# A two-layer hybrid encoder trunk on one core: output sums and combinations placed behind the newest low part on VectorE, ScalarE's final scalings spaced out, token tile 2 updated on VectorE

## The chip, the cores and the metric

The kernel runs on 1 core of one Trainium2 chip. The metric is device microseconds of an execution. TensorE (PE) multiplies, VectorE (DVE) and ScalarE (ACT) prepare operands and finish results, GpSimd (POOL) and SyncE (SP) mostly issue DMAs. Each engine takes its instructions strictly in the order in which they are queued on it.

## The reference

Two layers work on x of 512 tokens by 2048 features, float32. Cut to what matters:

```python
def hybrid_layer(x, w_in, w_out, g_pre, g_post, w_alpha, b_alpha, g_gla, g_att, rel_bias):
    h = rmsnorm(x, g_pre)
    z = h @ w_in                      # 2048 x 7184
    ...                               # gated linear attention, chunked attention, gates
    y = jnp.concatenate([o_gla, o_att], axis=-1) @ w_out     # 2048 x 2048
    return x + rmsnorm(y, g_post)

def reference(x, ...):
    h = x
    for l in range(2):
        h = hybrid_layer(h, w_in[l], w_out[l], ...)
    return h
```

The change concerns the output projection `@ w_out`, its RMS normalisation and the residual addition at the end of a layer.

## The kernel before

**Precision by splitting.** Every float32 operand is split into a high part (a cast to float32r) and a low part (the operand minus its high part). A product is three matmuls: high by high, high by low, low by high. For weights ScalarE makes the high part `wh` (line 191) and VectorE the low part `wl` (line 199). For activations and their sums the helper `split` does the same (cast at line 105 on ScalarE, low part at line 106 on VectorE).

**Seven products for eight.** Most projections use a Strassen-like scheme over 2 x 2 blocks with seven products P1 to P7 (`fast_gemm`). A projection of a pair of 512-column weight blocks is 28 jobs: a product and one of four chunks of 256 features, such as "52", product P5 of chunk 2. The order of the jobs is a list in the code; for the first output pair it is `PROD_OUT`. A job loads its weight block by a SyncE DMA (`raw` or `H`), some add or subtract two blocks on VectorE (lines 185 and 187), then `wh` and `wl` follow, and TensorE runs 12 matmuls of 128x512 (line 381). In the first output pair the jobs run 10 20 11 21 12 13 50 51 60 61 22 23 52 53 62 63 30 31 32 33 70 71 72 73 40 41 42 43. There are 4 buffers for `raw` and for `wh`, and 3 for `wl`.

**The other side's sums.** The products P5, P6, P3 and P7 need sums of activation blocks, named S1, S2, S4 and S3. For the output projection they are made by the generator `output_sums`: S1, S2 and S3 are differences (`sub`, line 1136), S4 is a sum (line 1153); `put` splits each (lines 105 and 106) and, in the last layer, GpSimd writes it to memory, from where the second output pair loads it again.

**Finishing.** As products complete, `combine` (line 338) forms an output block from accumulators and kept copies (line 333), and `project` squares it on ScalarE (line 1280) and multiplies it by the gain on VectorE (line 1281). After the second pair of the last layer `finish_token` does each of the four token tiles: a sum of squares (line 1296), a power on GpSimd (line 421), then the scaled result plus the residual `x_mid`. For tiles 0 and 1 and the first half of tile 2, ScalarE scales in place (line 1305), a GpSimd DMA adds `x_mid` into the tile (line 1306), and SyncE writes it out (line 1307). The second half of tile 2 and tile 3 are done by one VectorE instruction each piece (line 1311) and written from SyncE and ScalarE (line 1313).

**What sets the order.** Program text gives the dependencies; a scheduler in the framework, which works from its own estimate of times, sets the order on each engine. `tc.issue_after(x)` makes an instruction of the block stand behind x in the queue of x's own engine; it is an order, not a wait on a semaphore. `last_cast` holds the newest `wh` cast traced so far. Generators of side work are stepped from inside the matmul loops (`pump`), one step at a time.

Of the kernel before, what the change touches and what calls it, by code (L numbers as in the profile page):

```python
# [10 lines left out]
AF = mybir.ActivationFunctionType  # L11
ALU = mybir.AluOpType
# [21 lines left out]
def hybrid_trunk(  # L34
# [13 lines left out]
    nc = tc.nc  # L48
# [26 lines left out]
    def t2(shape=(512,), dtype=F32):  # L75
        return tmp.tile([P] + list(shape), dtype, tag="t2", name=nm("t2"))
# [55 lines left out]
    PROD_END = order("10 20 11 21 12 22 13 23 50 51 60 52 61 53 62 63 30 31 32 33 70 71 72 73 40 41 42 43")  # L132
    PROD_OUT = order("10 20 11 21 12 13 50 51 60 61 22 23 52 53 62 63 30 31 32 33 70 71 72 73 40 41 42 43")
    LEFT = {"P5": "S1", "P6": "S2", "P3": "S4", "P7": "S3", "P4": "A22"}
    last_cast = [None]

    class Job:
        def __init__(self, l, kind, c, b0, b1=None, pair=None):
# [57 lines left out]
        def low(self):  # L196
            self.wl = rtile("wl", dtype=F32R, bufs=3)
            for z in self.parts():
                nc.vector.tensor_tensor(  # L199
                    out=self.wl[:, z, :], in0=self.src[:, z, :], in1=self.wh[:, z, :].bitcast(F32), op=ALU.subtract  # L200
                )
            if self.kind == "P2" and self.b0 < NB_IN:
                h = self.pair["H", self.c]
                nc.vector.tensor_tensor(out=h, in0=h, in1=self.src, op=ALU.add)
# [483 lines left out]
    def layer(l):  # L688
        last = l == L - 1
# [416 lines left out]
        parts, gains = {}, []  # L1106
# [19 lines left out]
        def output_sums():  # L1126
            def put(name, i, src, tag=None):
                op = O[name, i] = slot(tag, [2, 512], F32R) if tag else rtile("sa", (2, 512), F32R)
                with tc.issue_after(last_cast[0]):
                    split(op[:, 0, :], op[:, 1, :], src)  # L1130
                if last:
                    nc.gpsimd.dma_start(so_d[name, OC[i]], flat(op))
                    written.add((id(so_d), name, OC[i]))

            def sub(dst, a, b):
                nc.vector.tensor_tensor(out=dst, in0=a, in1=b, op=ALU.subtract)

            for i0 in (0, 2):
                for name in ("S1", "S2"):
                    for i in (i0, i0 + 1):  # L1140
                        while (1, OC[i]) not in og:
                            yield
                        a11, _, a21, a22 = parts[OC[i]]
                        sub(a22, *((a21, a22) if name == "S1" else (a22, a11)))
                        put(name, i, a22, None if i0 else f"g{i + 2 * (name == 'S2')}")
                        yield
            for name in ("S4", "S3"):
                for i in range(4):
                    while (("P5", "P6")[i // 2], i % 2 + 2 * (name == "S3")) not in used or (0, OC[i]) not in og:
                        yield  # L1150
                    a11, a12, a21, a22 = parts[OC[i]]
                    if name == "S4":
                        nc.vector.tensor_tensor(out=a12, in0=a12, in1=a22, op=ALU.add)
                        put(name, i, a12, f"g{i}")
                    else:
                        sub(a11, a11, a21)
                        put(name, i, a11)
                    yield
# [135 lines left out]
        def finish_token(t, xs):  # L1294
# [5 lines left out]
            for i in range(D // step):  # L1300
                h, o = i * step // 1024, i * step % 1024
                yt = ys[t, h][:, o : o + step]
                rows = slice(t * P, (t + 1) * P), slice(i * step, (i + 1) * step)
                if last and (t < 2 or (t == 2 and i == 0)):
                    nc.scalar.activation(yt, yt, AF.Copy, scale=r)
                    nc.gpsimd.dma_start(yt, x_mid[rows], accum_op=ALU.add)
                    nc.sync.dma_start(out[rows], yt)
                else:
# [18 lines left out]
        def out_consume(n):  # L1327
# [4 lines left out]
            def f(j, h, t, src, comb):  # L1332
                until(lambda: len(gains) == 2)
                o = 2 * h + t
                project(o, n + j, comb(t2()), gains[j])
                if last and n == 2:
                    if (j, h, t) == (1, 0, 1):
                        tasks.append(finish(0, xs[0]))
# [82 lines left out]
```

## Time and profile before

| what | value |
|---|---|
| median of 3 runs | 1648.65 us (1648.48 to 1649.47) |
| the profiled execution | 1642.34 us, its span 1640.5 us |
| PE busy | 1617.2 us, 99% of the span |
| DVE busy | 1253.5 us, 76% |
| ACT busy | 909.7 us, 55% |
| granted TensorE clock, mean | 0.995 |

The page gives busy time by engine, the span in 40 slices, the queues, the chain that ended last and the costliest groups. In a timeline row stand start, length, engine, line, operation, output and inputs, and in brackets how long the engine stood idle before it and what ended that. Rows overlap a little: an instruction starts before the one ahead has drained, so the time one instruction takes of its engine is the distance from start to start. Layer 0's first output pair runs from about 648 to 731 us, layer 1's from about 1465 to 1548 us.

### The profile page before, as it was taken

The numbers are of one execution on the slowest core, as the hardware profiler recorded it, in microseconds if no ns is written. First come the engines' busy times: TensorE is split into PE (matmuls) and PEld (weight loads), VectorE is DVE, ScalarE is ACT, GpSimd is POOL, SyncE is SP. The second block draws the span as 40 slices with busy tenths as digits, with TensorE's granted clock in tenths as the row PEclk, the third lists the DMA queues.
The fourth block names the chain that finished last, engine by engine and source line by source line (L and its number), as shares of the span: only waits on it lengthen the run. The fifth ranks groups of instructions, "written<-read, shape, count | busy, mean of one in ns | idle before, by whom it ended". The sixth has DMA issues, their size and how long they took to land.

```text
span 1640.5 us, 24563 instructions
## 1 busy us (share of the span) xinstructions
PE 1617.2 (99%) x8986; PEld 1383.7 (84%) x8986; DVE 1253.5 (76%) x1635; ACT 909.7 (55%) x1498; POOL 134.2 (8%) x196
## 2 busy tenths in 40 slices
PE   9999999999999999999999999999999999999996
PEld 7888999998888778788888889999988877787885
DVE  5977677687787869985786576776777878699876
ACT  7554445566555456654784444455665545476554
POOL 0120000110100110000132000000000001101002
PEclk9999999999999999999999999999999999999998
DMA  9898685885859667486789486858758596786968
GB/s 345 270 357 293 221 302 199 266 298 173 307 192 339 225 220 267 145 296 214 240 282 394 172 311 218 298 189 273 269 183 291 184 327 235 241 282 246 345 224 269
DMA packets 130760, 426.70 MB, mean 260 GB/s; under 512 B 14084, under 2 KB 26756, under 8 KB 130640
## 3 DMA queue, kind: packets, MB, share of 16 engines
q1 hardware_dynamic: 113760, 366.09, 64.9%
q0 software_dynamic: 16304, 57.96, 9.7%
q8 instruction: 71, 1.16, 0.3%
q10 hardware_dynamic: 576, 1.08, 0.2%
q14 instruction: 49, 0.40, 0.1%
HBM read 371.84 MB, written 53.23 MB: 259 GB/s over the span
## 4 chain that ended last, share of the span: by engine, by line
PE 94%; DMA 2%; DVE 2%; issue 1%; ACT 0%; SPq 0%; DVEq 0%; POOL 0%; ACTq 0%
PE mm L381 47%; PE mm L371 19%; PE mm L302 16%; PE ax L891 2%; PE ax L381 2%; DMA raw<-in_w_dram 1%; PE ax L1072 1%; PE ax L874 1%; PE ax L711 1%; PE ax L1044 1%; DVE wl L199 1%; PE ax L855 1%; PE ax L854 1%; PE ax L853 1%; PE ax L1164 0%
## 5 line engine op out<-in xcount | busy, mean ns | idle before, releaser
L381 PE MATMUL mm<-wh,sa 128*128 128x512 f32 x1472 | 479.2, 396 | 1.2 <-ACT wh L191 1.0
L191 ACT CAST wh<-raw 128x1024 fp32r<-128x1024 f32 (+1 forms) x253 | 265.1, 1052 | 242.6 <-PE mm L381 65.2
L199 DVE TENSOR_TENSOR wl<-raw,wh 128x1024 fp32r<-128x1024 f32 (+1 forms) x253 | 306.5, 1216 | 92.7 <-PE mm L381 38.3
L191 ACT CAST wh<-H 128x1024 fp32r<-128x1024 f32 x240 | 251.4, 1050 | 214.8 <-PE mm L381 90.2
L199 DVE TENSOR_TENSOR wl<-H,wh 128x1024 fp32r<-128x1024 f32 x240 | 292.5, 1221 | 88.1 <-PE mm L381 35.8
L381 PEld LDWEIGHTS mm<-wh,sa 128*128 128x128 f32 x1472 | 277.5, 189 | 68.9 <-issue 7.9
L381 PE MATMUL mm<-wl,sa 128*128 128x512 f32 x736 | 289.6, 394 | 4.7 <-DVE wl L199 4.7
L371 PE MATMUL mm<-sa,wh 128*128 128x256 f32 x1280 | 236.7, 285 | 0.0
L381 PE MATMUL mm<-wh,a 128*128 128x512 f32 x608 | 200.5, 394 | 0.0
L371 PEld LDWEIGHTS mm<-sa,wh 128*128 128x128 f32 x1280 | 199.7, 191 | 0.1
L371 PE MATMUL mm<-sa,wl 128*128 128x256 f32 x640 | 181.2, 283 | 0.0
L381 PEld LDWEIGHTS mm<-wl,sa 128*128 128x128 f32 x736 | 139.1, 189 | 33.7 <-DVE wl L199 6.7
L185 DVE TENSOR_TENSOR H<-H,raw 128x1024 f32<-128x1024 f32 x132 | 160.2, 1219 | 8.1 <-DMA raw<-in_w_dram 7.0
L381 PEld LDWEIGHTS mm<-wh,a 128*128 128x128 f32 x608 | 113.2, 188 | 23.3
L187 DVE TENSOR_TENSOR raw<-H,raw 128x1024 f32<-128x1024 f32 x60 | 73.5, 1224 | 68.8 <-DMA raw<-in_w_dram 68.7
L371 PEld LDWEIGHTS mm<-sa,wl 128*128 128x128 f32 x640 | 122.5, 191 | 0.2
L421 POOL TENSOR_TENSOR sm<-sm,mhalf 128x2 f32<-128x2 f32 (+2 forms) x42 | 57.1, 1360 | 791.8 <-DVE sm L901 453.3
L381 PE MATMUL mm<-wl,a 128*128 128x512 f32 x304 | 119.8, 394 | 0.0
L371 PE MATMUL mm<-a,wh 128*128 128x256 f32 x512 | 95.2, 285 | 0.0
L302 PE MATMUL mm<-wh,a 128*128 128x512 f32 x288 | 91.7, 390 | 0.0
L381 PE MATMUL mm<-wh,g 128*128 128x512 f32 x288 | 90.8, 389 | 0.0
L333 ACT COPY ev<-mm 128x512 f32<-128x512 f32 x96 | 56.0, 583 | 56.3 <-PE mm L381 39.5
(237 smaller groups left out, 2428.5 us busy)
## 6 DMA issues: line engine op xcount, KB each, us to landing
raw<-in_w_dram SPq DMA_DIRECT2D x323, 512.0 KB, 4.8
sa<-S SPq DMA_DIRECT2D x184, 512.0 KB, 4.4
H<-in_w_dram SPq DMA_DIRECT2D x60, 512.0 KB, 4.6
sa<-A SPq DMA_DIRECT2D x48, 512.0 KB, 5.9
S<-g POOLq DMA_DIRECT2D x32, 512.0 KB, 9.0
sa<-oS SPq DMA_DIRECT2D x16, 512.0 KB, 4.5
oa<-g POOLq DMA_DIRECT2D x12, 512.0 KB, 6.6
bias<-in_rel_dram SPq DMA_DIRECT2D x16, 256.0 KB, 4.2
```

Source lines behind the costliest of these rows:

```text
L185: nc.vector.tensor_tensor(out=h, in0=h, in1=r, op=ALU.add)
L187: nc.vector.tensor_tensor(out=r, in0=h, in1=r, op=ALU.subtract)
L191: last_cast[0] = nc.scalar.copy(self.wh[:, z, :], src[:, z, :]).ins
L199: nc.vector.tensor_tensor(out=self.wl[:, z, :], in0=self.src[:, z, :], in1=self.wh[:, z, :].bitcast(F32), op=ALU.subtract)
L302: nc.tensor.matmul(pss[o], a(part, kk, o) if callable(a) else a[:, part, t], rhs[:, kk, :], start=(i == 0 and kk == 0 and m == 0), stop=(i ...
L333: nc.scalar.copy(e, src[t])
L371: nc.tensor.matmul(dst, lhs[:, kk, f], a[:, part, tok], start=(fresh and kk == 0 and m == 0 and ft % 2 == 0), stop=(c == 3 and kk == 1 and ...
L381: nc.tensor.matmul(out_ps[t], a[:, part, tok], rhs[:, kk, :], start=(fresh and kk == 0 and m == 0), stop=(c == 3 and kk == 1 and m == 2), ...
L421: nc.gpsimd.tensor_tensor(out=out_r, in0=v, in1=mhalf[:, : v.shape[-1]], op=ALU.pow)
L711: nc.tensor.matmul(ps[0:96, half * 256 : (half + 1) * 256], wga[kt // 10][:, kt % 10, :], op[:, i, (kt % 2) * 256 : (kt % 2 + 1) * 256], s ...
L853: nc.tensor.matmul(ps[:, :n], self.qh[:, t], self.kh[:, :n], start=True, stop=False)
L891: nc.tensor.matmul(o, self.pt[i][:, j * P : (j + 1) * P], av[hd // 4, j // 2][:, j % 2, (hd % 4) * P : (hd % 4 + 1) * P], start=(j == 0), ...
```

## The change

Five edits. `last_low` records the newest weight low part traced (line 199). The differences and sums of `output_sums` and their low parts are queued on VectorE behind it. So are the combination and the product with the gain, in both output pairs that use `fast_gemm`, except for the last products of the very last pair. In the last layer the scalings of tiles 0 and 1 on ScalarE are each traced three steps later and queued behind the newest cast. The first half of tile 2 is updated on VectorE like the rest of it, without the accumulating DMA.

```diff
-    last_cast = [None]
+    last_cast, last_low = [None], [None]
...
         def low(self):
             self.wl = rtile("wl", dtype=F32R, bufs=3)
             for z in self.parts():
-                nc.vector.tensor_tensor(
+                last_low[0] = nc.vector.tensor_tensor(
                     out=self.wl[:, z, :], in0=self.src[:, z, :], in1=self.wh[:, z, :].bitcast(F32), op=ALU.subtract
-                )
+                ).ins
...
-                with tc.issue_after(last_cast[0]):
+                with tc.issue_after(last_cast[0]), tc.issue_after(last_low[0]):
                     split(op[:, 0, :], op[:, 1, :], src)
...
-            def sub(dst, a, b):
-                nc.vector.tensor_tensor(out=dst, in0=a, in1=b, op=ALU.subtract)
+            def sub(dst, a, b, op=ALU.subtract):
+                with tc.issue_after(last_low[0]):
+                    nc.vector.tensor_tensor(out=dst, in0=a, in1=b, op=op)
...
-                        nc.vector.tensor_tensor(out=a12, in0=a12, in1=a22, op=ALU.add)
+                        sub(a12, a12, a22, ALU.add)
...
-                if last and (t < 2 or (t == 2 and i == 0)):
-                    nc.scalar.activation(yt, yt, AF.Copy, scale=r)
+                if last and t < 2:
+                    for _ in range(3):
+                        yield
+                    with tc.issue_after(last_cast[0]):
+                        nc.scalar.activation(yt, yt, AF.Copy, scale=r)
                     nc.gpsimd.dma_start(yt, x_mid[rows], accum_op=ALU.add)
                     nc.sync.dma_start(out[rows], yt)
...
                 o = 2 * h + t
-                project(o, n + j, comb(t2()), gains[j])
+                with tc.issue_after(last_low[0]) if n == 0 or (j, h) != (0, 1) else nullcontext():
+                    project(o, n + j, comb(t2()), gains[j])
```

The scheduler moves rows over the whole of both output pairs. On VectorE in layer 0, from the low part of job 23 (wl_6857) to that of job 52 (wl_6880), the order before is this. H_6609 and H_6649 are the blocks of jobs 52 and 53, raw_6839 and raw_6862 what is added to them; L1153 is an S4 sum, L1136 here an S3 difference, L106 a sum's low part, L338 and L1281 a combination and its product with the gain:

```order
L199 TENSOR_TENSOR wl_6857<-raw_6817,wh_6837 128x1024
L106 TENSOR_TENSOR g_1313_6842<-g_1208_6328,g_1313_6842 128x512
L106 TENSOR_TENSOR sa_6771<-g_1251_6556,sa_6771 128x512
L1153 TENSOR_TENSOR t_1253_6560<-t_1253_6560,t_1255_6562 128x512
L1136 TENSOR_TENSOR t_1252_6559<-t_1252_6559,t_1254_6561 128x512
L106 TENSOR_TENSOR sa_6775<-t_1255_6562,sa_6775 128x512
L185 TENSOR_TENSOR H_6609<-H_6609,raw_6839 128x1024
L338 TENSOR_TENSOR t_1327_6927<-ax_6661,ev_6797 128x512
L185 TENSOR_TENSOR H_6649<-H_6649,raw_6862 128x1024
L1281 TENSOR_TENSOR a_1329_6931<-t_1327_6927,bias_6743 128x512
L338 TENSOR_TENSOR t_1331_6935<-ax_6662,ev_6799 128x512
L199 TENSOR_TENSOR wl_6880<-H_6609,wh_6860 128x1024
```

And now, between the same two low parts (all differences and sums now have line 1137):

```order
L199 TENSOR_TENSOR wl_6857<-raw_6817,wh_6837 128x1024
L1137 TENSOR_TENSOR g_1250_6555<-g_1250_6555,g_1251_6556 128x512
L106 TENSOR_TENSOR g_1313_6842<-g_1208_6328,g_1313_6842 128x512
L106 TENSOR_TENSOR sa_6771<-g_1251_6556,sa_6771 128x512
L185 TENSOR_TENSOR H_6609<-H_6609,raw_6839 128x1024
L106 TENSOR_TENSOR sa_6775<-t_1255_6562,sa_6775 128x512
L185 TENSOR_TENSOR H_6649<-H_6649,raw_6862 128x1024
L199 TENSOR_TENSOR wl_6880<-H_6609,wh_6860 128x1024
```

The two combinations, the product, the last S4 sum and the S3 difference went behind wl_6880; an S4 sum (g_1250) that stood ahead of wl_6857 came in between. Three more S3 differences that stood ahead of wl_6857 went behind wl_6880. Layer 1 moves likewise.

At the end of the program VectorE's last rows were these (L1296 sums the squares of tiles 2 and 3, L1311 updates tile 2's second half, g_2946, and tile 3, bias and sg):

```order
L1296 TENSOR_REDUCE sm_15743<-ssy_15025 128x1
L1311 SCALAR_TENSOR_TENSOR g_2946_15118<-g_3063_15665,sm_15717,g_2946_15118 128x1024
L1311 SCALAR_TENSOR_TENSOR bias_15121<-g_2925_15027,sm_15744,bias_15121 128x512
L1311 SCALAR_TENSOR_TENSOR bias_15122<-g_2925_15027,sm_15744,bias_15122 128x512
L1311 SCALAR_TENSOR_TENSOR sg_15123<-g_3066_15671,sm_15744,sg_15123 128x512
L1311 SCALAR_TENSOR_TENSOR sg_15124<-g_3066_15671,sm_15744,sg_15124 128x512
```

Now one more row heads them, tile 2's first half (g_2945):

```order
L1297 TENSOR_REDUCE sm_15743<-ssy_15025 128x1
L1315 SCALAR_TENSOR_TENSOR g_2945_15117<-g_2921_15019,sm_15717,g_2945_15117 128x1024
L1315 SCALAR_TENSOR_TENSOR g_2946_15118<-g_3063_15659,sm_15717,g_2946_15118 128x1024
L1315 SCALAR_TENSOR_TENSOR bias_15121<-g_2925_15027,sm_15744,bias_15121 128x512
L1315 SCALAR_TENSOR_TENSOR bias_15122<-g_2925_15027,sm_15744,bias_15122 128x512
L1315 SCALAR_TENSOR_TENSOR sg_15123<-g_3066_15665,sm_15744,sg_15123 128x512
L1315 SCALAR_TENSOR_TENSOR sg_15124<-g_3066_15665,sm_15744,sg_15124 128x512
```

On ScalarE, shortly before, the four scalings of tiles 0 and 1 (line 1305) stood around one cast:

```order
L1305 ACTIVATE a_2868_14747<-a_2868_14747,sm_15570 128x1024
L1305 ACTIVATE g_2991_15303<-g_2991_15303,sm_15570 128x1024
L191 CAST wh_15623<-H_15069 128x1024
L1305 ACTIVATE a_2872_14755<-a_2872_14755,sm_15599 128x1024
L1305 ACTIVATE g_2994_15309<-g_2994_15309,sm_15599 128x1024
```

Now three casts stand among them:

```order
L1309 ACTIVATE a_2868_14747<-a_2868_14747,sm_15570 128x1024
L191 CAST wh_15610<-H_15069 128x1024
L1309 ACTIVATE g_2991_15303<-g_2991_15303,sm_15570 128x1024
L191 CAST wh_15632<-H_15105 128x1024
L191 CAST wh_15655<-H_15173 128x1024
L1309 ACTIVATE a_2872_14755<-a_2872_14755,sm_15637 128x1024
L1309 ACTIVATE g_2994_15309<-g_2994_15309,sm_15637 128x1024
```

The last two casts came forward past the scalings of tile 1, one past the second scaling of tile 0.

## The prediction

> **What bounds the kernel now.** I read the page's head first, then the list of waits of TensorE, then the timelines around the waits, and last the end of the program.
>
> ```profile
> span 1640.5 us, 24563 instructions
> PE   9999999999999999999999999999999999999996
> PE mm L381 <- DVE wl L199: 5.0, 3, 2.3
> PE mm L381 <- ACT wh L191: 1.0, 2, 0.5
> ```
>
> TensorE is busy in every slice but the last, and its waits on the two weight-preparing engines sum to only 6.0 us. So an edit on VectorE or ScalarE can pay in two places only: at those waits, and in the last slice, where TensorE has ended. The timeline of TensorE has the waits, once in each layer, at the same instruction (job 52 of the first output pair: its high part comes late, then its low part):
>
> ```profile
> 682.21 0.39 PE L381 MATMUL ax<-wh,a 128*128 128x512 f32 x1
> 683.11 0.73 PE L381 MATMUL mm<-wh,sa 128*128 128x512 f32 x2 [0.51 <-ACT wh L191]
> 686.17 0.50 PE L381 MATMUL mm<-wl,sa 128*128 128x512 f32 x1 [2.33 <-DVE wl L199]
> ...
> 1502.90 0.50 PE L381 MATMUL mm<-wl,sa 128*128 128x512 f32 x1 [2.33 <-DVE wl L199]
> ```
>
> Each costs more than its 0.51 + 2.33 = 2.84 us. The table by short windows (busy time of the engines, then granted clock, DMA share, GB/s) shows the clock at half just after:
>
> ```profile
> 687.00:688.00 1.00, 1.00 (x5) 0.83 (x4) 1.00 (x2) 0.00 (x0) 0.00 (x0) 0.85 0.13 53
> 688.00:689.00 1.00, 1.00 (x4) 0.75 (x3) 1.00 (x3) 0.00 (x0) 0.00 (x0) 0.50 0.00 0
> ...
> 691.00:692.00 1.00, 1.00 (x6) 0.80 (x5) 0.95 (x2) 0.91 (x2) 0.00 (x0) 0.95 0.00 0
> ...
> 1504.00:1505.00 1.00, 1.00 (x4) 0.81 (x3) 1.00 (x2) 0.00 (x0) 0.53 (x1) 0.50 0.61 246
> 641.00:690.00 49.00, 46.16 (x206) 37.58 (x205) 48.94 (x66) 28.85 (x48) 2.71 (x5) 0.98 0.47 153
> 690.00:731.00 41.00, 40.99 (x177) 33.13 (x177) 36.25 (x38) 25.12 (x35) 2.13 (x4) 0.99 0.71 248
> ```
>
> The clock is lost from about 687.8 to 691.1 us, so 0.15 + 3 x 0.50 + 0.05 = 1.7 us more: 4.5 us for each layer. The last two rows give the cause: in the 49 us up to the wait VectorE (third busy figure) works 48.94 us, in the 41 us behind it only 36.25. Too much short work stands ahead of the late low part, and there is room for it behind.
>
> **The change: VectorE's new order in the first output pair.** One row of each kind has its time here, from VectorE's timeline in layer 0:
>
> ```profile
> 676.53 1.22 DVE L199 TENSOR_TENSOR wl<-raw,wh 128x1024 fp32r<-128x1024 f32 x1
> 677.67 0.69 DVE L106 TENSOR_TENSOR g<-g,g 128x512 fp32r<-128x512 f32 x1
> 678.27 0.69 DVE L106 TENSOR_TENSOR sa<-g,sa 128x512 fp32r<-128x512 f32 x1
> ...
> 680.68 1.22 DVE L185 TENSOR_TENSOR H<-H,raw 128x1024 f32<-128x1024 f32 x1
> ...
> 682.57 1.22 DVE L185 TENSOR_TENSOR H<-H,raw 128x1024 f32<-128x1024 f32 x1
> ...
> 684.90 1.22 DVE L199 TENSOR_TENSOR wl<-H,wh 128x1024 fp32r<-128x1024 f32 x1
> ```
>
> From start to start a 1024-wide row takes 677.67 - 676.53 = 1.14 us and a 512-wide one 678.27 - 677.67 = 0.60. The change adds or removes no work here; it moves rows. By the two orders eight 512-wide rows that stood ahead of wl_6880 (the row at 684.90) now stand behind it: one S4 sum, four S3 differences, two combinations and one product with the gain. By the queue alone the low part would come 8 x 0.60 = 4.8 us earlier, at 680.1 us, and TensorE, which wants it two matmuls after 682.44 (at 682.9), would not wait.
>
> The queue alone does not decide. The addition for job 53 (682.57) stands ahead of wl_6880 in both orders, and needs a weight whose transfer starts when an earlier low part frees the buffer. The DMA issues, and from single issues' answers the time to landing, for those at 681.93, 1498.66 and 1500.54 us in this order:
>
> ```profile
> 677.78 0.33 SPq L149 DMA_DIRECT2D raw<-in_w_dram  x1
> 681.93 0.33 SPq L149 DMA_DIRECT2D raw<-in_w_dram  x1
> DMA to landing us min/median/max: 4.5/4.5/4.5
> DMA to landing us min/median/max: 7.3/7.3/7.3
> DMA to landing us min/median/max: 6.4/6.4/6.4
> ```
>
> The issue at 677.78 follows the end of wl_6857 (676.53 + 1.22). That low part has four short rows fewer ahead of it (2.4 us), but low parts have three buffers, so one can't start before TensorE is through with the job three before, and VectorE now reaches two of them too early. I count 0.5 us earlier, with 0 and 2.4 as bounds: transfer issued at 677.3, landed 4.5 us later at 681.8, addition to 682.9, low part to 684.1 with its signal. TensorE then waits some 1.2 us where it waited 2.84. The next job that can be late is 62. Job 52's addition has six short rows fewer ahead (3.6 us), less the 1.9 us of waiting just counted: 1.7 us earlier, so the transfer behind it issues at 680.2, and the one behind job 53's addition at 682.9; that lands at 687.4, addition to 688.6, low part to 689.7. When TensorE asked for it before:
>
> ```profile
> 693.35 0.39 PE L381 MATMUL mm<-wl,sa 128*128 128x512 f32 x1
> 1506.01 2.36 DVE L185 TENSOR_TENSOR H<-H,raw 128x1024 f32<-128x1024 f32 x2 [0.21 <-DMA raw<-in_w_dram]
> 1508.42 2.37 DVE L199 TENSOR_TENSOR wl<-H,wh 128x1024 fp32r<-128x1024 f32 x2
> 1510.09 0.39 PE L381 MATMUL mm<-wl,sa 128*128 128x512 f32 x1
> ```
>
> So layer 0 is 693.35 - 689.7 = 3.6 us ahead there; VectorE must then fit the postponed sums between the additions, with 41.0 - 36.25 = 4.8 us of room, of which I let 0.6 us come back as small waits: **3.0 us**. Bounds: 4.5 (all of it) and 1.3 (the remaining waits halve the clock again, 1.7 us).
>
> In layer 1 the same transfer took 7.3 us, and VectorE waited for it at 1506.01. Job 62's low part ended about 1508.42 + 1.2 = 1509.6, half a microsecond before TensorE wanted it: this chain was next in line. It moves by the same 1.7 us and no more, so 1.7 us is the gain at job 62; its waits sum to more, about 2 us, and I add half the price of a halved clock, 0.85 us, against it. Later short waits on low parts in this layer (the third of the three counted in the first fence) give 0.5 us back: **1.4 us**, between 0 (the clock halves) and 5.1.
>
> The Trainium skill, "TensorE: Matmul & The Clock Gate", section "HAM oscillation — how this bites in real kernels", names idle gaps above about 3.4 us as what throttles the clock. The trace differs: two idle stretches of 0.51 and 2.33 us were enough in both layers. By the page no remaining wait would cost clock, and layer 1's term would be 0.85 us larger; I go by the rows.
>
> **The change at the end.** TensorE's last matmul, and what follows it on VectorE, ScalarE, GpSimd and SyncE, with three transfers' times to landing:
>
> ```profile
> 1624.61 0.39 PE L381 MATMUL mm<-wh,g 128*128 128x512 f32 x1
> 1627.18 1.28 DVE L1311 SCALAR_TENSOR_TENSOR g<-g,sm,g 128x1024 f32<-128x1024 f32 x1 [0.17 <-POOL sm L421]
> 1628.38 1.41 DVE L1311 SCALAR_TENSOR_TENSOR bias<-g,sm,bias 128x512 f32<-128x512 f32 x2
> 1629.70 1.41 DVE L1311 SCALAR_TENSOR_TENSOR sg<-g,sm,sg 128x512 f32<-128x512 f32 x2
> 1627.18 1.15 ACT L1305 ACTIVATE g<-g,sm 128x1024 f32<-128x1024 f32 x1 [0.43 <-POOL sm L421]
> 1628.70 0.88 POOL L1306 DMA_DIRECT2D g<-x_mid  x1 [1.04 <-ACT g L1305]
> 1636.66 0.33 SPq L1307 DMA_DIRECT2D out_dram<-g  x1
> g<-x_mid POOLq DMA_DIRECT2D x1, 512.0 KB, 7.9
> out_dram<-g SPq DMA_DIRECT2D x1, 512.0 KB, 3.1
> out_dram<-sg SPq DMA_DIRECT2D x1, 256.0 KB, 6.8
> ```
>
> The last output leaves at 1636.66 because its half tile goes scaling, accumulating transfer (7.9 us), then output. The change takes scaling and transfer away and puts one update of 1.20 us (1628.38 - 1627.18) at the head of VectorE's final five, whose last ends at 1629.70 + 1.41 = 1631.1. The six end at 1632.3, and the last output issues at 1632.4. Landing takes 3.1 to 6.8 us; the 6.8 was beside the accumulating transfer, so I take 4.3: end at 1636.7 instead of 1640.5, **3.8 us**, bounds 1.3 and 5.0. The spaced scalings of tiles 0 and 1 let casts pass first, three where one stood between them. Their transfers start later by at most two casts, each about as long as the scaling quoted (1.15 us), which TensorE's last stretch covers: I cost it at nothing, 2.3 us if that cover is gone. The list of waits names no wait of TensorE there, so the earlier casts gain nothing either.
>
> **The sum.** 3.0 + 1.4 + 3.8 = 8.2 us. The profiled execution took 1642.34 us (span 1640.5 and 1.8 around it) and would take 1634.1; the median of the runs shown is 1648.65, 6.3 us above it, and the same gain gives **1640.4**.
>
> **Rivals.** *All waits vanish*: the orders put every low part early enough and transfers land sooner. Then 4.5 + 4.5 + 0.5 + 3.8 = 13.3 us, 1635.4. For it: 36.25 of 41 us on VectorE behind the wait. Against: the 7.3 us landing and the 0.21 us wait on it. *Given back*: job 62's transfers take the place of job 52's queue and the clock halves again; only the end pays, 1644.8. For it: that chain's half microsecond of slack in layer 1. *Slower*: a sum queued behind the newest low part has to wait until TensorE frees that part's buffer, and TensorE then waits for the sum as its operand. Sum, cast and low part are about 0.6 each, 1.9 us; with two such operands in each layer 7.6 us, with two halved clocks 3.4 more, less the 3.8 at the end, beside today's waits: 1655.9, with one in each layer and no clock 1648.7. It decides once an operand's low part stands behind the weight's low part of its own job; in the new order sa_6711, job 52's operand, is followed by the low parts of two other jobs before job 52's own, which speaks against it. *Nothing moves*: TensorE's waits are replaced one for one, and the end stays bound by DMA traffic, whose share after the last matmul is the number before the last in this window's row: within 3 us of before.
>
> ```profile
> 1632.00:1633.00 1.00, 0.00 (x0) 0.00 (x0) 0.00 (x0) 0.00 (x0) 0.00 (x0) 0.50 1.09 227
> ```
>
> **How the numbers follow.** Forecast 0.55, all waits vanish 0.20, given back 0.12, slower 0.07, nothing 0.06. The range 1634.5 to 1645.5 takes in the first three: its low edge is all waits gone with 0.9 us more at the end, its high edge the end's gain alone, 0.6 us short. No change means within 0.2% here, 3.3 us, about what a measurement of this kernel can tell. Faster: 0.55 + 0.20 + most of 0.12, 0.86. Same: 0.07, slower: 0.07.
>
> **What would show it.** Right: TensorE's wait at job 52 is near 1 us or gone, a wait on a low or high part appears at job 62 of layer 1 with a weight's DMA behind it, the granted clock stays at 1.00 in layer 0, GpSimd has four accumulating transfers and the last output is issued about 7.5 us after the last matmul. Wrong: TensorE waits on a sum's operand; job 52's low part is on time and nothing else is late (then I mis-sized the transfers' chain); or the end stays above 14 us with the last output issued early.

## The result, and the profile after

| | before | changed |
|---|---|---|
| median, first comparison (7 runs each) | 1648.48 us (1644.33 to 1649.79) | 1641.05 us (1638.92 to 1645.92) |
| ratio, first comparison | | 0.9967, 95% interval 0.9953 to 0.9980 |
| median, second comparison (25 and 12 runs) | 1646.84 us (1642.31 to 1649.21) | 1642.04 us (1639.91 to 1647.44) |
| ratio, second comparison | | 0.9977, 95% interval 0.9965 to 0.9989 |
| the profiled execution | 1642.34 us, span 1640.5 us | 1641.22 us, span 1639.5 us |

The change makes the kernel faster by about 0.28%, the mean of the two ratios: 4.6 us. The medians of the first comparison are 7.4 us apart; its seven runs of before have a higher median than the 25 of the second. The two profiled executions are only 1.1 us apart: the one of before lay below all timed runs shown with it.

The head of the page of the changed kernel and its list of TensorE's waits: TensorE is as full as it was, and the low parts it waits for are more in number, not fewer.

```profile
span 1639.5 us, 24568 instructions
PE   9999999999999999999999999999999999999996
PE mm L381 <- DVE wl L199: 5.6, 8, 2.2
PE mm L302 <- ACT wh L191: 0.5, 1, 0.5
```

In the first output pairs of the changed kernel TensorE no longer has a long wait in layer 0. The first row is the longest of three there (the others are 0.28 and 0.42 us); the next four are those of layer 1:

```profile
690.30 0.50 PE L381 MATMUL mm<-wl,sa 128*128 128x512 f32 x1 [0.61 <-DVE wl L199]
1501.36 0.50 PE L381 MATMUL mm<-wl,sa 128*128 128x512 f32 x1 [2.18 <-DVE wl L199]
1507.86 0.50 PE L381 MATMUL mm<-wl,sa 128*128 128x512 f32 x1 [0.53 <-DVE wl L199]
1528.30 0.50 PE L381 MATMUL mm<-wl,sa 128*128 128x512 f32 x1 [0.94 <-DVE wl L199]
1537.16 0.50 PE L381 MATMUL mm<-wl,g 128*128 128x512 f32 x1 [0.39 <-DVE wl L199]
```

The stall of job 52 is gone in layer 0; in layer 1 2.18 us of its 2.84 are left. What VectorE and ScalarE did ahead of that row, in the changed kernel's timeline (job 52's addition, its cast, job 53's addition, job 52's low part), and the windows of layer 0 and layer 1 that hold the same jobs (busy time of the engines, clock, DMA share, GB/s):

```profile
1495.45 1.23 DVE L185 TENSOR_TENSOR H<-H,raw 128x1024 f32<-128x1024 f32 x1
1496.79 1.05 ACT L191 CAST wh<-H 128x1024 fp32r<-128x1024 f32 x1 [4.16 <-DVE H L185]
1498.94 1.23 DVE L185 TENSOR_TENSOR H<-H,raw 128x1024 f32<-128x1024 f32 x1 [2.27 <-DMA raw<-in_w_dram]
1500.09 1.22 DVE L199 TENSOR_TENSOR wl<-H,wh 128x1024 fp32r<-128x1024 f32 x1
...
678.00:693.00 15.00, 14.39 (x63) 11.23 (x62) 14.89 (x18) 8.61 (x11) 0.00 (x0) 1.00 0.33 105
1495.00:1510.00 15.00, 12.29 (x52) 9.29 (x51) 12.59 (x14) 7.75 (x10) 2.25 (x5) 1.00 0.76 291
```

VectorE stands idle for 2.27 us at job 53's addition, whose weight has not landed, and job 52's low part, whose cast had ended at 1496.79 + 1.05 = 1497.8 us, is queued behind it. That weight's transfer was issued at 1493.12 us (5.8 us ahead), and DMA carried 291 GB/s in the window shown; in layer 0, at 105 GB/s, the same transfer was issued at 677.91 and its addition began at 681.54, 3.6 us later, without a pause. Layer 1's traffic alone is not the reason: in the kernel before the same weight of layer 1 landed 3.9 us after its issue (experiment e3_nosums).

At the end of the changed kernel the last output is issued where the prediction had it, and the DMA engines are full (the number before the last) from before the last matmul to 1636 us:

```profile
1632.16 1.20 SPq L1317 DMA_DIRECT2D out_dram<-sg  x1
...
1618.00:1622.00 4.00, 4.00 (x20) 3.30 (x19) 3.14 (x5) 3.58 (x8) 1.71 (x2) 1.00 1.03 183
1624.00:1626.00 2.00, 0.37 (x2) 0.00 (x0) 1.97 (x5) 1.32 (x4) 0.48 (x1) 1.00 1.05 256
1632.00:1634.00 2.00, 0.00 (x0) 0.00 (x0) 0.00 (x0) 0.00 (x0) 0.00 (x0) 0.50 1.02 410
1636.00:1638.00 2.00, 0.00 (x0) 0.00 (x0) 0.00 (x0) 0.00 (x0) 0.00 (x0) 0.50 0.55 209
```

### The stages of all profiled executions

One pair of profiles could not show where 4.6 us went, so the table has all fourteen. Lengths are in us, worked out from TensorE's rows: a first output pair runs from its first row at line 381 into `ax` (651.27 us in before, layer 0) to the first row of what follows (731.75; in layer 1 from 1468.00 to the second pair's first row at 1549.13); the second pair runs to the end of the last matmul, the tail from there to the end of the span. "Half clock" counts the stretches of 3.41 us at half clock in these three pairs (e1_end had one more between the first two). The labels are those of the experiments below.

| execution | pair, layer 0 | pair, layer 1 | second pair | tail | half clock |
|---|---|---|---|---|---|
| before | 80.48 | 81.13 | 75.87 | 15.54 | 1, 1, 0 |
| e1_before | 79.71 | 81.33 | 80.17 | 14.80 | 0, 1, 1 |
| e1_end | 81.19 | 82.65 | 76.30 | 14.67 | 2, 1, 0 |
| changed | 77.69 | 80.97 | 76.01 | 15.08 | 0, 0, 0 |
| e2_after | 77.79 | 80.94 | 76.72 | 14.65 | 0, 0, 0 |
| e1_order | 78.23 | 82.02 | 77.09 | 15.25 | 0, 1, 0 |
| e1_nospace | 77.95 | 83.06 | 80.41 | 13.20 | 0, 1, 0 |
| e2_noaccum | 77.63 | 82.53 | 76.16 | 11.88 | 0, 1, 0 |
| e2_sums | 80.95 | 83.83 | 77.71 | 15.08 | 0, 0, 0 |
| e2_addlow | 85.04 | 84.01 | 81.34 | 13.77 | 0, 0, 0 |
| e3_nosums | 78.13 | 80.87 | 76.55 | 14.59 | 0, 0, 0 |
| e3_one53 | 78.16 | 84.45 | 75.87 | 14.19 | 0, 2, 0 |
| e3_t1 | 78.07 | 82.63 | 76.24 | 11.78 | 0, 1, 0 |
| e4_best | 78.13 | 82.83 | 77.34 | 11.80 | 0, 1, 0 |

By groups: with the old order (before, e1_before, e1_end) the pair takes 80.46 us in layer 0 and 81.70 in layer 1; with the new one (changed, e2_after, e1_order, e1_nospace, e2_noaccum, e3_t1) 77.89 and 82.03. So 2.6 us are gained in layer 0 and 0.3 lost in layer 1. The second pair takes 78.25 us where the scalings are not spaced (before, e1_before, e1_order, e1_nospace, e2_sums) and 76.27 where they are (changed, e2_after, e1_end, e2_noaccum, e3_nosums, e3_one53): 2.0 gained. The tail takes 15.17 us with the old end (before, e1_before, e1_order, e2_sums) and 14.64 with the changed one (changed, e2_after, e1_end, e3_nosums, e3_one53): 0.5 gained. The sum is 2.6 - 0.3 + 2.0 + 0.5 = 4.8 us, against 4.6 by the timed runs.

Each profile is one draw, so look at the spread too. In layer 0 the two groups do not overlap (79.71 to 81.19 against 77.63 to 78.23). In layer 1 they do (81.13 to 82.65 against 80.94 to 83.06), so the 0.3 us is not told apart from nothing; the tails overlap as well. In the second pair the group without spacing runs from 75.87 to 80.41 us, the one with it from 75.87 to 76.72. The rest of the program, which the table leaves out, takes 1387.5 to 1393.0 us in the fourteen, a wider spread than the gain; so the sum's close agreement is in part chance.

The timed runs show another side of the gain. One stretch of 3.41 us at half clock costs 1.7 us and lowers the mean granted clock of an execution by 1.7 / 1645 = 0.001. In the second comparison the 25 runs of before have a mean clock of 0.9943 and the 12 of the changed kernel 0.9965. By this estimate the changed kernel has about two such stretches fewer, worth 3.6 us.

### The profile page after: what moved, and what is told of

The parts are those of the page before. It is cut to its first block, busy times and chain, and to the rows that moved or that the text cites. A ratio compares the mean times of both kernels' runs of the same rounds, so it can differ in the third digit from the quotient of the medians.

```text
span 1639.5 us, 24568 instructions
## 1 busy us (share of the span) xinstructions
PE 1615.8 (99%) x8986; PEld 1380.7 (84%) x8986; DVE 1255.0 (77%) x1636; ACT 909.9 (56%) x1497; POOL 130.6 (8%) x195
## 4 chain that ended last, share of the span: by engine, by line
PE 90%; DMA 4%; DVE 3%; issue 1%; ACT 0%; DVEq 0%; POOL 0%; SPq 0%; ACTq 0%
PE mm L381 44%; PE mm L371 18%; PE mm L302 16%; DMA raw<-in_w_dram 3%; PE ax L891 2%; DVE wl L199 2%; PE ax L381 2%; PE ax L1072 1%; PE ax L874 1%; PE ax L711 1%; PE ax L1044 1%; DMA sa<-S 1%; PE ax L855 1%; PE ax L854 1%; PE ax L853 1%
```

## The experiments

Ratios are to the kernel before, run on the same chip, each with its 95% interval.

**e1_before: the kernel before once more.** No edit.

> The kernel before, unchanged, profiled once more. Forecast's view: the profiled execution of before was ordinary, so a second profile has the same two stalls (0.51 + 2.33 us at job 52 in each layer, each followed by 3.4 us at half clock), a mean granted clock near 0.995 in the timed runs too, and a time of 1642 to 1649 us that varies by waits spread over the kernel. Rival: the profiled execution was a lucky one, and timed runs of before have more halved clocks, some four more of 1.7 us each to make up 6.3 us: mean granted clock 0.991 to 0.993 in the slower runs.

Measured: 1646.87 us, ratio 1.0005 (0.9995 to 1.0014); granted clock 0.992 to 0.996 in its runs. Its profile has the same stall at job 52 in both layers, and one at the end that the first profile lacked. ScalarE's and TensorE's rows there, then windows behind the stall of job 52 in layer 0 (where TensorE waited 0.51 + 2.33 us again) and behind the one at the end:

```profile
1618.09 1.16 ACT L1305 ACTIVATE a<-a,sm 128x1024 f32<-128x1024 f32 x1 [1.70 <-POOL sm L421]
1619.15 1.14 ACT L1305 ACTIVATE g<-g,sm 128x1024 f32<-128x1024 f32 x1
1620.19 1.98 ACT L191 CAST wh<-H 128x1024 fp32r<-128x1024 f32 x2
...
1621.27 0.73 PE L381 MATMUL mm<-wh,g 128*128 128x512 f32 x2 [0.97 <-ACT wh L191]
1622.53 0.57 PE L381 MATMUL mm<-wl,g 128*128 128x512 f32 x1 [0.53 <-DVE wl L199]
...
688.00:689.00 1.00, 1.00 (x6) 0.84 (x5) 1.00 (x3) 0.00 (x0) 0.00 (x0) 1.00 0.00 0
1623.00:1624.00 1.00, 1.00 (x4) 0.81 (x3) 1.00 (x3) 0.49 (x2) 0.00 (x0) 0.50 1.00 262
```

The casts of the last two weights stand behind tile 1's scalings, and these wait 1.70 us for GpSimd's power. TensorE waits 0.97 + 0.53 us and loses half the clock for 3.4 us: 3.2 us. What follows: before's profile was one draw. It missed a stall that the spaced scalings remove, and it showed a halved clock in layer 0 that the same wait did not bring here.

**e1_order: VectorE's order alone.** The changed kernel with the end of the kernel before:

```diff
-                if last and t < 2:
-                    for _ in range(3):
-                        yield
-                    with tc.issue_after(last_cast[0]):
-                        nc.scalar.activation(yt, yt, AF.Copy, scale=r)
+                if last and (t < 2 or (t == 2 and i == 0)):
+                    nc.scalar.activation(yt, yt, AF.Copy, scale=r)
```

> Only VectorE's new order (sums and combinations behind the newest low part); scalings and tile 2 as before. Forecast's terms: 3.0 + 1.4 = 4.4 us faster than before, ratio 0.9973. Rival, from where TensorE's rows stand in the two profiles: 2.2 us gained in layer 0's first output pair, nothing in layer 1's, so 1.8 to 2.5 us, ratio 0.9987. If this alone gives the 7 us between the medians, the new order also removes stalls that the profile of before did not show.

Measured: 1645.23 us, ratio 0.9989 (0.9977 to 1.0000): 1.8 us, as the rival had it; the interval reaches from nothing to 3.8 us and leaves the forecast's 4.4 out. Layer 0's pair took 78.23 us, layer 1's 82.02 with a wait of 1.78 us and a halved clock.

**e1_end: the two edits at the end alone.** The kernel before with the lines that e1_order takes out.

> Only the two edits at the end (scalings spaced, tile 2 on VectorE); VectorE's order in the output pairs as before. Forecast's term: 3.8 us faster than before, ratio 0.9977, span end 12 us after the last matmul. Rival: the end is bound by DMA traffic, whose share is at 1.0 from 1618 to 1636 us in the changed kernel, so 0 to 1 us, ratio 0.9994 to 1.0, end still 15 us after the last matmul.

Measured: 1643.91 us, ratio 0.9982 (0.9973 to 0.9991), 3.0 us: nearer to the forecast's size, but not where it was forecast. The tail is 14.67 us, as the rival says; no wait of TensorE stands behind 1610 us, which fits the stall shown in e1_before being gone. That stall is in some executions of the kernel before and not in others, so this profile alone does not show it.

**e1_nospace: the changed kernel without the spacing.**

```diff
                 if last and t < 2:
-                    for _ in range(3):
-                        yield
-                    with tc.issue_after(last_cast[0]):
-                        nc.scalar.activation(yt, yt, AF.Copy, scale=r)
+                    nc.scalar.activation(yt, yt, AF.Copy, scale=r)
```

> The changed kernel with the scalings of tiles 0 and 1 where they were before (not spaced), tile 2 still on VectorE. Forecast's view: spacing costs nothing and brings nothing, same time as the changed kernel (ratio to before 0.9967). Rival: the spacing makes the accumulating transfers start later (1613.6, 1616.7, 1618.7, 1619.6 us against 1612.5, 1613.6, 1616.7, 1617.6), DMA has idle time before them and is full behind them, so without the spacing the end comes 1 to 2 us earlier, 13 to 14 us after the last matmul, ratio to before 0.9955 to 0.9961.

Measured: 1643.74 us, ratio 0.9979 (0.9966 to 0.9993); the timed runs do not tell it from the changed kernel. In its profile TensorE waits 1.01 + 0.52 us for casts and a low part at 1625 us, which no profile of the group with spaced scalings has. The tail is 13.20 us, 1.4 shorter than that group's, in the rival's range, but this does not show the rival: the 1.53 us of waiting lie between the last accumulating transfer and the last matmul, and bring the end nearer to the last matmul by as much. Counted from the start of the second pair the program ends after 80.41 + 13.20 = 93.6 us, and after 90.1 to 91.4 with spaced scalings and the same four accumulating transfers. Of the 93.6, 1.7 us are two waits for sums that are loaded again from memory; they stand ahead of the scalings, so the spacing has no part in them.

**e2_after: the changed kernel once more.** No edit.

> The changed kernel unchanged, profiled and timed once more beside the others. Theory now (order 1.8 to 2 us, end 2.9 us, the latter mostly a stall of TensorE before casts that wait behind the scalings and that the profile of before happened not to have): ratio to before about 0.997, mean granted clock about 0.9965 against 0.994 of before, no wait of TensorE between 1610 and 1630 us. Rival (the first comparison was a lucky draw of few runs): ratio 0.9985 or above.

Measured: 1642.04 us, ratio 0.9977 (0.9965 to 0.9989), between the two. The waits of the first profile come again, within 0.2 us each: 0.63 at job 62 of layer 0; 2.06, 0.53, 0.86 and 0.56 in layer 1.

**e2_sums: of the new order only the sums.** The changed kernel with the old end, and:

```diff
-                with tc.issue_after(last_low[0]) if n == 0 or (j, h) != (0, 1) else nullcontext():
-                    project(o, n + j, comb(t2()), gains[j])
+                project(o, n + j, comb(t2()), gains[j])
```

> Of VectorE's new order only the sums and their low parts behind the newest low part; combinations and products with the gain, scalings and tile 2 as before. The order alone gave 0.9989. If the sums are what stood ahead of job 52's low part: the same 0.9989, and the stall of 0.51 + 2.33 us at job 52 gone in layer 0. If the combinations (two and one product ahead of job 52's low part, 1.8 us) carry it: stall at job 52 of layer 0 still over 1 us and ratio 0.9995 to 1.0.

Measured: 1649.39 us, ratio 1.0017 (1.0007 to 1.0027): slower, which neither side expected. The stall at job 52 of layer 0 is gone, so moving the sums was enough there; but it comes back two jobs later, at job 62:

```profile
687.71 0.68 DVE L1282 TENSOR_TENSOR a<-t,bias 128x512 f32<-128x512 f32 x1
688.31 0.68 DVE L338 TENSOR_TENSOR t<-ax,ev 128x512 f32<-128x512 f32 x1
...
690.64 1.21 DVE L199 TENSOR_TENSOR wl<-H,wh 128x1024 fp32r<-128x1024 f32 x1
...
691.91 0.50 PE L381 MATMUL mm<-wl,sa 128*128 128x512 f32 x1 [2.14 <-DVE wl L199]
```

The combinations and the product now stand ahead of job 62's low part, which starts at 690.64 us instead of 689.03 in the changed kernel. Moving half of the short work moves the stall by two jobs. In layer 1 TensorE waits 2.73 us at job 52, and the pair takes 83.83 us.

**e2_addlow: weight additions behind the newest low part too.** The changed kernel, and:

```diff
+                with tc.issue_after(last_low[0]) if self.b0 == NB_IN else nullcontext():
                     if k in ("P5", "P6") or (k == "P4" and self.b0 >= NB_IN):
                         nc.vector.tensor_tensor(out=h, in0=h, in1=r, op=ALU.add)
```

> The changed kernel, and the additions and subtractions of weight blocks of the first output pair also stand behind the newest low part, so job 52's low part stands ahead of job 53's addition. Theory: in layer 1 of the changed kernel VectorE idles 2.27 us at that addition for a weight's DMA while job 52's low part, whose input is there, stands behind it, and TensorE waits 2.18 us; now this wait is gone (under 0.3 us), and 1.5 to 3 us are gained against the changed kernel, ratio to before 0.9950 to 0.9958. Rival (the transfers are late for every job, so the wait only moves to job 53 or 62): TensorE's waits between 1498 and 1512 us still sum to 2 us or more and the ratio stays at that of the changed kernel.

Measured: 1653.97 us, ratio 1.0046 (1.0030 to 1.0062); my theory fell. VectorE's and ScalarE's rows of one job (addition, cast, low part), and TensorE's:

```profile
684.69 1.22 DVE L186 TENSOR_TENSOR H<-H,raw 128x1024 f32<-128x1024 f32 x1
...
686.02 1.05 ACT L192 CAST wh<-H 128x1024 fp32r<-128x1024 f32 x1 [1.98 <-DVE H L186]
...
687.10 1.23 DVE L200 TENSOR_TENSOR wl<-H,wh 128x1024 fp32r<-128x1024 f32 x1
688.25 1.22 DVE L186 TENSOR_TENSOR H<-H,raw 128x1024 f32<-128x1024 f32 x1
...
684.83 0.50 PE L382 MATMUL mm<-wl,sa 128*128 128x512 f32 x1 [0.52 <-DVE wl L200]
688.38 0.50 PE L382 MATMUL mm<-wl,sa 128*128 128x512 f32 x1 [0.52 <-DVE wl L200]
691.93 0.51 PE L382 MATMUL mm<-wl,sa 128*128 128x512 f32 x1 [0.51 <-DVE wl L200]
```

From addition to addition 688.25 - 684.69 = 3.56 us pass, and TensorE's low parts come 3.55 us apart, where its 12 matmuls need 2.72. The next addition (688.25) stands behind this job's low part, which needs its cast, which needs its own addition: one job at a time. The additions that stand ahead of a low part, and that I blamed, are what lets two jobs overlap.

**e2_noaccum: no accumulating transfers for tiles 0 and 1.** The residual is left out of these two tiles.

```diff
-                    nc.gpsimd.dma_start(yt, x_mid[rows], accum_op=ALU.add)
```

> The changed kernel with the four accumulating transfers of tiles 0 and 1 left out, so that the residual is not added in these two tiles. If the end is bound by DMA traffic (2 MB by accumulating transfers at some 210 GB/s): DMA share falls below 0.8 before the last matmul, last output issued 7.5 to 8 us after the last matmul as in the changed kernel, end 11.5 to 12.5 us after it instead of 15.1, some 3 us faster than the changed kernel. If not (the end is the landing of the last outputs alone): end still 14 to 15 us after the last matmul.

Measured: 1640.53 us, ratio 0.9965 (0.9951 to 0.9979). The tail is 11.88 us. The windows around the last matmul:

```profile
1620.00:1624.00 4.00, 4.00 (x18) 3.01 (x16) 1.70 (x4) 1.46 (x4) 0.00 (x0) 1.00 0.13 49
1624.00:1628.00 4.00, 0.03 (x1) 0.00 (x0) 3.72 (x7) 1.18 (x4) 1.53 (x2) 1.00 0.00 0
1628.00:1632.00 4.00, 0.00 (x0) 0.00 (x0) 3.32 (x5) 0.00 (x0) 0.00 (x0) 0.63 0.93 363
```

The DMA engines are empty when the last tiles are ready, and the tail is 2.8 us shorter than the group's 14.64. The last output is issued 7.3 us behind the last matmul, near the changed kernel's 7.8, but the program ends 4.6 us behind it instead of 7.3. So the changed kernel's end is bound by DMA traffic that the accumulating transfers bring or hold back. The run does not separate the two: tile 1's outputs, twice 512 KB, no longer have to wait for an accumulating transfer and leave before the last matmul, where the changed kernel issues them 2.1 and 5.4 us behind it. At the 410 GB/s of its last windows they take 2.6 us by estimate, nearly all of the difference.

**e3_nosums: the changed kernel without its sums part.**

```diff
-                with tc.issue_after(last_cast[0]), tc.issue_after(last_low[0]):
+                with tc.issue_after(last_cast[0]):
...
-                with tc.issue_after(last_low[0]):
-                    nc.vector.tensor_tensor(out=dst, in0=a, in1=b, op=op)
+                nc.vector.tensor_tensor(out=dst, in0=a, in1=b, op=op)
```

> The changed kernel without its sums part: only the combinations and products stand behind the newest low part, and the end as changed. The sums alone made the kernel 0.17% slower (1.0017) while both together gave 0.9989, so the combinations are worth some 0.28%, 4.6 us, on top of the sums. If the two parts simply add: ratio to before 0.9954 + about 0.0, that is 1.7 x 10^-3 below the changed kernel's 0.9972, 2.8 us faster than it. Rival (each undoes what the other leaves late): the sums still stand ahead of job 52's low part, only 1.8 us of short rows are gone of 2.84 us of waiting, TensorE waits about 1 us there in each layer, and the time is the changed kernel's or 1 to 2 us more.

Measured: 1641.84 us, ratio 0.9966 (0.9953 to 0.9978), not told apart from the changed kernel by time. TensorE's waits at job 52 of layer 1 are what the rival said; VectorE's two additions stand first:

```profile
1495.55 2.35 DVE L185 TENSOR_TENSOR H<-H,raw 128x1024 f32<-128x1024 f32 x2
...
1497.98 0.73 PE L381 MATMUL mm<-wh,sa 128*128 128x512 f32 x2 [0.51 <-ACT wh L191]
1499.24 0.50 PE L381 MATMUL mm<-wl,sa 128*128 128x512 f32 x1 [0.53 <-DVE wl L199]
1505.78 0.50 PE L381 MATMUL mm<-wl,sa 128*128 128x512 f32 x1 [0.53 <-DVE wl L199]
```

They are 1.04 us in place of 2.18, and VectorE makes both additions without a pause. They come 1.4 us later in the pair (29.4 us from its start instead of 28.05), but above all the weight of job 53 lands sooner. Its time from issue to landing in layer 1, in before, in the changed kernel and here; then GpSimd's writes of two sums, in before and in the changed kernel:

```profile
DMA to landing us min/median/max: 3.9/3.9/3.9
DMA to landing us min/median/max: 5.8/5.8/5.8
DMA to landing us min/median/max: 3.8/3.8/3.8
...
1486.64 0.54 POOL L1132 DMA_DIRECT2D oS<-sa  x1 [9.79 <-DVE sa L106]
1488.37 0.54 POOL L1132 DMA_DIRECT2D oS<-sa  x1 [1.19 <-DVE sa L106]
...
1488.38 1.08 POOL L1132 DMA_DIRECT2D oS<-sa  x2 [10.12 <-DVE sa L106]
```

In before the two writes are issued 1.7 us apart, the first 18.6 us into the pair; in the changed kernel they go back to back, 21.0 us into it, and the weight follows at 25.7. Of the profiles other than e2_addlow, the eight with the sums moved (e2_sums among them) have this weight land 5.1 to 5.8 us after its issue, the five without (before, e1_before, e1_end, e3_nosums, e4_best) 3.5 to 3.9. So moving the sums makes the weight late in the layer where they are written to memory. That the writes' traffic is the link is argued from these times; no run left the writes out.

The combinations carry the gain of the order; the sums' part brings nothing that the timed runs can see.

**e3_one53: one addition behind one low part, in layer 1.** The condition of e2_addlow cut down to job 53 of the last layer.

> The changed kernel, and in layer 1 alone job 53's addition stands behind job 52's low part (one instruction's place; what the scheduler makes of it elsewhere follows). When every addition stood behind the newest low part, addition, cast and low part of each job ran one after the other, 3.55 us a job against TensorE's 2.72. Theory: one such place costs that chain once at most and takes away the 2.06 to 2.18 us wait at job 52, of which 0.5 to 1 us comes back at jobs 53 and 62: 1 to 1.6 us faster than the changed kernel, ratio 0.9963 to 0.9968. Rival: the weight's late landing then delays job 53 by the same 2 us: same time as the changed kernel.

Measured: 1643.69 us, ratio 0.9980 (0.9969 to 0.9992), the rival's time. The wait at job 52 is gone and one job later it is twice as long:

```profile
1497.88 1.22 DVE L186 TENSOR_TENSOR H<-H,raw 128x1024 f32<-128x1024 f32 x1
...
1502.96 1.23 DVE L186 TENSOR_TENSOR H<-H,raw 128x1024 f32<-128x1024 f32 x1 [2.67 <-DMA raw<-in_w_dram]
...
1504.11 1.22 DVE L200 TENSOR_TENSOR wl<-H,wh 128x1024 fp32r<-128x1024 f32 x1
...
1505.39 1.22 PE L382 MATMUL mm<-wh,sa 128*128 128x512 f32 x2 [4.36 <-ACT wh L192]
```

The scheduler put job 62's addition (1502.96) ahead of job 53's low part (1504.11), and now that addition waits for its weight. The wait is put down to a cast, but its end, 1505.39 us, is that of the low part, 1504.11 + 1.22 = 1505.33; job 53's cast had long been done. The clock halves for two stretches behind it. The next weight is late too, so this changed order only picked which low part stands behind it. (The trace has no record of the low part's first matmul in that job, so the wait stands at the row after it.) A fifth weight buffer, which would let the transfers start earlier, was not tried.

**e3_t1: tile 1 updated on VectorE as well.** The changed kernel, and its residual is loaded by SyncE into two weight buffers:

```diff
+            if last and t == 1:
+                xs = [rtile("raw") for _ in range(2)]
+                for h, z in enumerate(xs):
+                    nc.sync.dma_start(flat(z), x_mid[t * P : (t + 1) * P, h * 1024 : (h + 1) * 1024])
+                xs = [flat(z) for z in xs]
...
-                if last and t < 2:
+                if last and t < 1:
```

The two updates are each traced three steps later and queued behind the newest low part.

> The changed kernel with token tile 1 of the last layer also updated on VectorE: its residual is loaded by two plain SyncE transfers into two weight buffers that are free by then, so 1 MB of accumulating transfers becomes 1 MB of plain ones, and two scalings leave ScalarE. Theory (the end is bound by DMA traffic; without any accumulating transfer it ended 11.9 us after the last matmul, with four 14.7 to 15.1): about half of the 3 us, end 12.5 to 13.5 us after the last matmul, no wait of TensorE after 1600 us, 1 to 2 us faster than the changed kernel, ratio about 0.9962. Rival (VectorE has no room: two updates of 1.13 us delay the last combinations): TensorE's end is the same but the last outputs issue 9.5 to 10 us after it and nothing is gained.

Measured: 1639.16 us, ratio 0.9953 (0.9939 to 0.9966), some 3 us faster than the changed kernel's mean ratio; the intervals of the two kernels overlap a little. The last output and the windows of the end:

```profile
1636.13 0.33 SPq L1325 DMA_DIRECT2D out_dram<-sg  x1
...
1629.00:1633.00 4.00, 0.42 (x2) 0.00 (x0) 3.66 (x8) 1.52 (x5) 1.46 (x2) 1.00 0.62 248
1633.00:1637.00 4.00, 0.00 (x0) 0.00 (x0) 3.76 (x5) 0.00 (x0) 0.00 (x0) 0.63 0.82 322
```

The last matmul ended at 1629.4, the last output issues 6.7 us behind it, DMA has room, and the tail is 11.78 us. No wait of TensorE stands behind 1600 us: with two scalings fewer on ScalarE the casts pass.

**e4_best: e3_nosums and e3_t1 together.**

> Both findings together: combinations behind the newest low part, sums not; tile 1 as well as tile 2 updated on VectorE, its residual by plain transfers. Theory (the two lie in different stages and add): the changed kernel's 0.9972, less 0.0006 to 0.0010 for the sums, less 0.0019 for the tile, so ratio 0.9943 to 0.9948, about 1638 us; end 11.5 to 12.5 us after the last matmul; TensorE's waits at job 52 about 1 us in each layer and no halved clock there. Rival (the sums part was neutral, its difference noise of few runs): the ratio of the kernel with tile 1 on VectorE, 0.9953.

Measured: 1640.56 us, ratio 0.9962 (0.9947 to 0.9977), five runs. Both marks are there (1.04 us at job 52 in each layer, tail 11.80 us), yet in its profile layer 1 has another wait, of 1.65 us for a cast at job 62, and a halved clock. No better than e3_t1, which stays the fastest kernel that was run, and leaves nothing of the result out.

## Why the prediction was right, and where it was not

The forecast of 1640.4 us lies 0.65 us from the first median, and faster was right. That it came so near is luck: two parts of it were both too large, and cancelled, a gain of 8.2 us, where 4.6 to 4.8 were there, taken off a median of 1648.65 us from three runs, where larger sets of runs of before gave 1645.89 (35 runs) to 1647.44 (17).

- **Layer 0's first pair, 3.0 us: right.** 2.6 us by the stages. The wait at job 52 is gone (I had 1.2 us left), 0.6 us came back at job 62 in all profiles of the new order, and in the changed kernel 0.7 in two shorter waits. The sign "the granted clock stays at 1.00 in layer 0" held in every one.
- **Layer 1's first pair, 1.4 us: wrong, nothing gained (-0.3, inside the spread).** The step that failed is "It moves by the same 1.7 us and no more". The 1.7 us were worked out in layer 0, with job 53's weight "landed 4.5 us later", as if the change left that time alone. It did not: in layer 1 that weight landed 3.9 us after its issue in before and needs 5.8 us in the changed kernel, because the sums were moved, and most likely by way of GpSimd's writes that move with them (e3_nosums). The short work taken out of VectorE's queue then only lets VectorE wait longer, and 1.5 to 2.2 us of TensorE's wait at job 52 stay in the six profiles of the new order. That the additions stand ahead of job 52's low part was seen; that the change moves a landing, and not only a queue, was not. The later waits (0.53, 0.94, 0.39) sum to 1.9 us, and the half chance of a halved clock is near: four of the six have one in this pair.
- **The end, 3.8 us: wrong, 0.5 in the tail.** The last output was issued at 1632.2 us as worked out (1632.4). The step that failed is "landing takes 3.1 to 6.8 us ... so I take 4.3": the program ended 7.3 us behind that issue. The row quoted for the rival "nothing moves", a DMA share of 1.09 behind the last matmul, was the decisive one; e2_noaccum shows the tail at 11.9 us without the accumulating transfers. The bounds (1.3 to 5.0) did not reach to it. Of the prediction's own signs of being wrong this one came: the end stayed above 14 us (15.1) with the last output issued early, 7.8 us behind the last matmul.
- **Spaced scalings, nothing: wrong, some 1.5 us gained.** "The list of waits names no wait of TensorE there, so the earlier casts gain nothing" rests on one profile. Of the five without spacing the other four have waits behind the scalings, of 0.42 to 1.7 us, one with a halved clock; of the six with it none has. The groups differ by 2.0 us in the second pair; 0.5 of it are waits for loads of sums in e1_nospace and e2_sums, ahead of the scalings. Whether "which TensorE's last stretch covers" held for the later transfers stays open: the shorter tail of e1_nospace, the one run without them, is explained by TensorE's own wait there.
- **The rivals.** None came true as a whole. *Nothing moves* was right that the end stays bound by DMA traffic. *Slower*, a sum behind a low part that waits, did not occur: in the changed kernel's output pairs TensorE waits for low parts alone.

## What to carry to other kernels

An order of short work ahead of a critical instruction is worth what its inputs' arrival allows: look whether the row that ends the wait stands behind another that waits for a DMA, and in each layer anew, since the traffic differs. Work that is moved takes along the transfers that are issued behind it: here moving the sums made a weight's transfer 1.9 us longer. Keep the next job's addition ahead of this job's low part when a third engine's cast lies between them, or the jobs run one at a time. Before costing the last transfers by their own landing time read the DMA share of the windows ahead of them, and before costing a cover at nothing look at a second profile.

## What the runs showed of the hardware

**The clock halves by a fixed period.** All records of a halved clock ahead of the last matmul last 3.413 us or a multiple, and within one execution they start whole multiples of 3.4133 us apart, the one that begins behind the last matmul too: 239 periods between the two in before, 35 in e1_before, 193 and 48 in e1_end. Cutting TensorE's idle time (behind the start-up) along this period in the fourteen profiles: every period with 1.78 us or more of it, twelve in all, was followed by one at half clock; of those with less, one was (1.50 us, e1_before at 1622.8), and periods with 1.77, 1.76 and 1.65 us were not. Once at half, 0.66 and 1.54 us kept it there for another. So the same stall of 2.33 us costs 1.7 us more or nothing by where it falls against the period, as in e1_before in layer 0. The Trainium skill, "TensorE: Matmul & The Clock Gate", section "HAM oscillation — how this bites in real kernels", gives idle gaps above some 3.4 us as the bound; no gap here but one (4.36 us) was that long, and the measurement decides.

**Accumulating transfers fill the DMA engines at about half the rate.** In the changed kernel the windows with accumulating transfers show a share of 1.03 to 1.05 at 183 to 256 GB/s; with plain outputs alone 1.02 at 410 GB/s.
